# The last row of the last forgetting pair: squares moved by transfers between SBUF partitions instead of turns on TensorE

## The chip, the cores and the metric

The kernel runs on one core of a Trainium2 chip. A core has five engines with a queue of instructions each: TensorE (PE) for matrix products, VectorE (DVE), ScalarE (ACT), GpSimd (POOL) and SyncE (SP), which issues most transfers. Each engine takes its instructions in order and waits on semaphores for the others. Matrix products land in PSUM banks; everything else lies in SBUF, 128 partitions wide. The metric is the device time of one execution in microseconds.

## The reference

One layer of a streaming-encoder trunk on 512 tokens of 1024 channels in float32: four parallel token mixers, cross-attention into 256 memory tokens, and a gated MLP. The four mixers read one normalized input, their outputs are projected, gated and summed. The change touches mixer B, the forgetting attention with 8 heads of 64 channels:

```python
log_f = jax.nn.log_sigmoid(f_g + b_fgt)
c = jnp.cumsum(log_f, axis=1)
s = jnp.einsum('bqhd,bkhd->bhqk', q_blk, k) * scale
s = s + c_blk[..., None] - c_k[:, :, None, :]
p = jax.nn.softmax(jnp.where(mask, s, -jnp.inf), axis=-1)   # mask: key not later than query
o = jnp.einsum('bhqk,bkhd->bqhd', p, v)
```

The scores and the softmax have the queries on the partitions and the keys along the row. The product with the values sums over the keys, so TensorE needs the probabilities with the keys on the partitions. Turning them over, block by block, is what the change is about.

## The kernel before

Everything that stays exact to float32 is computed with split operands: a value is cut into a high half (a rounded copy, ScalarE) and a low half (the rest, VectorE), and a product is three matmuls, high by high, high by low and low by high (`mm3`). Weights go the same way: a raw tile `wr` (two buffers) is loaded by SyncE, split into `wh` and `wl` (four buffers each), lines 201 and 202, and used by one job. `run_blocks` goes through a list of jobs and emits the load and split of a job's weights three jobs ahead of its products.

The eight heads are done in four pairs. `f_task` of a pair is a generator with numbered steps. Steps 0 to 3 each do one row of 128 queries for both heads: scores on TensorE into two PSUM banks (`ps_sc`), the bias added on VectorE, the exponential on ScalarE, the scaling by the reciprocal sum (line 1141 on VectorE for one head, line 1143 on ScalarE for the other). Row r has (r + 1) times 128 keys. Tiles `e` with three buffers hold these rows and also their turned copies.

A row is turned in one of two ways:

- By way of DRAM. `turn_squares` transposes each 32 by 32 square in place of its block (VectorE, line 857), `put` writes the tile to DRAM (line 862), and `get` reads it back with block rows and partitions exchanged (line 869), which puts the keys on the partitions. The result lands in the low half's tile, and `split_in_place` (lines 875 and 876) cuts it into the tiles `pth` and `ptl`. All rows go this way but one.
- By the identity. `to_keys_major` turns each 128 by 128 block by a matrix product with the identity on TensorE (line 250, bank `ps_tr`), and `split` (lines 164 and 165) cuts the bank into the two tiles. Only row 3 of the last pair goes this way, in step 4.

`values` (in two halves, rows 0 and 1, then rows 2 and 3) multiplies the turned probabilities with the values into two banks `ps_av`; then lines 1155 and 1156 add the two parts and a split writes the pair's slice of the tile `y`, which the last branch reads. For rows 0 and 1 of the last pair the turned tiles are named `half`.

The order of the work: the list of jobs sets the order in which the program emits its main work. Background tasks such as `f_task` are advanced by a planner between blocks of matmuls: a step has a cost that is paid out of a credit, and a due time (its rest) before which the next step isn't taken. At the end of the mixer jobs `bg.drain("f")` takes all steps still left one after the other, whatever their rests. The pairs wait for each other: the last pair's step 4 waits until the pair before has done step 7. The compiler's scheduler then orders each engine's queue by its own timeline, so jobs that are emitted later can fill an engine while a step waits. After the drain come the jobs of the last branch: two gates (products of the normalized input with gate weights, tile names `hth` and `htl`), then a branch product with `y`, and so on in that rhythm. A PSUM bank for a job is taken in turn from a list of tags; `share_now("mm")` in step 4 of the last pair takes the bank `tr0` out of that list so that the turns can have it, and a later `share("mm", "av")` sets the list anew.

Of the kernel before, what the change touches and what calls it, by code (L numbers as in the profile page):

```python
# [17 lines left out]
F32 = mybir.dt.float32  # L18
# [68 lines left out]
def hybrid_layer(ctx: ExitStack, tc: tile.TileContext, a: dict, out: bass.AP):  # L87
    nc = tc.nc
    V, A, G, PE, SP = nc.vector, nc.scalar, nc.gpsimd, nc.tensor, nc.sync
# [10 lines left out]
    def bank(tag=None):  # L100
        if tag is None:
            turn_of.n += 1
            tag = turn_of.among[turn_of.n % len(turn_of.among)]
        elif tag == "tr":
            turn_of.tr = 1 if "tr0" in turn_of.among else 1 - turn_of.tr
            tag = f"tr{turn_of.tr}"
        return psum.tile([P, 512], F32, tag=tag, name=f"ps_{tag}", bufs=1 if tag[:2] == "tr" else 2)

    def share_now(*among):
        vars(turn_of).update(n=1, among=among)  # L110
# [29 lines left out]
    for i in range(8):  # L140
        n = ("wh", "wl")[i % 2]
# [3 lines left out]
        elif i < 6:  # L145
            n = ("fz_raw", "fz", "fe", "fu", "fd")[i - 1]
# [14 lines left out]
    def split(ps, hi, lo, scale=None):  # L161

        if scale is None:
            A.copy(hi, ps)  # L164
            V.tensor_tensor(lo, ps, hi.bitcast(F32), ALU.subtract)
        else:
            A.activation(hi, ps, AF.Copy if isinstance(scale, float) else AF.Identity, scale=scale)
            V.scalar_tensor_tensor(lo, ps, scale, hi.bitcast(F32), ALU.mult, ALU.subtract)
# [80 lines left out]
    def transpose(ps, x, n=P):  # L249
        turns.append(PE.transpose(ps, x, ident[:n, :n]).ins)  # L250
        bg.clock += 0.107
# [137 lines left out]
    for i, plan in enumerate(plans):  # L389
        r_t = m1p.tile([P, P], F32, tag="fbias" if i == 2 else "ck", name=f"rows{i}", bufs=2)  # L390
        n = 0
# [45 lines left out]
    turned = {}  # L437
# [401 lines left out]
    def to_keys_major(e, n, pt, local):  # L839

        ps = bank("tr")
        for kt in range(n):
            transpose(ps[:, kt * P:(kt + 1) * P], e[:, kt * P:(kt + 1) * P])
        split(ps[:, :n * P].rearrange("p (t a i) -> p a t i", t=n, a=4), *(x[:, local, :, :n] for x in pt))
# [14 lines left out]
    def put(e, w):  # L859
        d = dram.tile([2, P * S], F32, tag="turned", name="turned", bufs=6)[:e.shape[1], :P * w]  # L860
        d = d.rearrange("h (p x) -> p h x", p=P)
        SP.dma_start(d, e[:, :, :w])
        return d

    def part_of(pt, n, local):
        return pt[:, local, :, :n].rearrange("p a t i -> p a (t i)")

    def get(d, n, pt, local):
        SP.dma_start(part_of(pt[1], n, local).bitcast(F32), d.rearrange("(a j) (b x) -> (j b) a x", j=32, b=4))

    def split_in_place(n, pt, local):
        hi, lo = (part_of(x, n, local) for x in pt)
        raw = lo.bitcast(F32)
        with tc.issue_after(evacuations[0]):
            A.copy(hi, raw)  # L875
        V.tensor_tensor(lo, raw, hi.bitcast(F32), ALU.subtract)  # L876
# [24 lines left out]
    GETS, SPLITS = {3: (0, 1), 5: (2, 3)}, {4: (0, 1), 6: (2, 3)}  # L901
# [151 lines left out]
    def f_task(p, qk, v):  # L1053
        f_steps[p] = 0
        last = p == 3
        while f_steps[p - 1] < 4:
            yield 0.0, 0.5
        ck = []
        for j in range(2):
            t = m1p.tile([P, S], F32, tag="ck", name="ck", bufs=2)  # L1060
            G.dma_start(t, crows[2 * p + j:2 * p + j + 1, :].rearrange("a s -> (a s)").partition_broadcast(P))
            ck.append(t)
        yield 0.0, 2.0 if p else 5.0
        if "f" not in y:
            y["f"] = (y8(), y8())
        es, pts, av, ready = {}, {}, None, []
        gets, splits, rests, ends = ({4: (2,)}, {4: (0, 1), 5: (2,)}, {3: 2.0}, (5, 6)) if last else (GETS, SPLITS, {5: 6.5}, (5, 7))

        def fetch(qt):
            d = es.pop(qt)  # L1070
            for j in range(2):
                get(d[:, j], qt + 1, pts[qt // 2][j], qt % 2)

        def own_tiles():

            free = m1p.tile([P, 6, S], F32R, tag="qk", name="half", bufs=2)
            return [tuple(free[:, 2 * j + i].rearrange("p (l a t i) -> p l a t i", l=2, a=4, t=2) for i in range(2))
                    for j in range(2)]

        def turn_ready():  # L1080
            while ready:
                qt, e, w = ready.pop()
                turned = e4()
                for j in range(2):
                    turn_squares(turned[:, j, :w], e[:, j, :w])
                es[qt] = put(turned, w)
        for step in range(ends[1] + 1):
            if step in ends:
                if av is None:
                    av = [bank("av"), bank("av")]  # L1090
                with tc.issue_after(steps_of[0]):
                    for j in range(2):
                        hl = v[0][:, :, 2 * p + j]
                        half = ends.index(step)
                        values(av[j], lambda kt: ((hl[:, kt], 0), (hl[:, kt], 1)), pts[half][j], half)
            while step == (4 if last else 3) and f_steps[p - 1] < 8:
                yield 0.0, 0.5
            f_steps[p] = step + 1
            cost = 0.0
            if step == 4:  # L1100
                turn_ready()
            for qt in splits.get(step, ()):
                for j in range(2):
                    split_in_place(qt + 1, pts[qt // 2][j], qt % 2)
                cost += 0.1 + 0.3 * qt
            for qt in gets.get(step, ()):
                if qt % 2 == 0:
                    pts[qt // 2] = [pt_tiles() for _ in range(2)]
                fetch(qt)
            if step == 4 and last:  # L1110
                share_now("mm")
                e = es.pop(3)
                for j in range(2):
                    to_keys_major(e[:, j], 4, pts[1][j], 1)
                cost += 1.3
            if step < 4:
                qt, w = step, (step + 1) * P
                e = es[qt] = e4()
                st = m1p.tile([P, 8], F32, tag="st8", name="st8", bufs=4)
                for j in range(2):  # L1120
                    head = 2 * p + j
                    bias = m1p.tile([P, S], F32, tag="fbias", name="fbias", bufs=2)

                    G.tensor_scalar(bias[:, :w], ck[j][:, :w], -1.0, cq[:, qt, head:head + 1],
                                    ALU.mult, ALU.add)
                    G.affine_select(out=bias[:, w - P:w], in_=bias[:, w - P:w], pattern=[[-1, P]],
                                    compare_op=ALU.is_ge, fill=BIG, base=0, channel_multiplier=1)
                    ps = bank("sc")
                    scores(ps, qk, j, qt * P, w)
                    low = V.tensor_tensor_reduce(e[:, j, :w], ps[:, :w], bias[:, :w], scale=-HD ** -0.5,  # L1130
                                                 scalar=3.0e38, op0=ALU.add, op1=ALU.min,
                                                 accum_out=st[:, j:j + 1])
                with tc.issue_after(low.ins):
                    turn_ready()
                for j in range(2):
                    A.activation(e[:, j, :w], e[:, j, :w], AF.Exp, bias=st[:, j:j + 1],
                                 scale=-1.0, accum_out=st[:, 4 + j:5 + j])
                V.reciprocal(st[:, 6:8], st[:, 4:6])
                for j in range(2):
                    if j:  # L1140
                        V.tensor_scalar(e[:, j, :w], e[:, j, :w], st[:, 6 + j:7 + j], None, ALU.mult)
                    else:
                        A.activation(e[:, j, :w], e[:, j, :w], AF.Copy, scale=st[:, 6 + j:7 + j])
                cost += 0.6 + 0.0038 * w
                if not last or qt < 3:
                    ready.append((qt, e, w))
                    cost += 0.003 * w
                if last and qt == 2:
                    pts[0] = own_tiles()
                    fetch(0)  # L1150
                    fetch(1)
            yield cost, rests.get(step, 4.5)
        e = e4()
        for j in range(2):
            A.copy(e[0:HD, j], av[j][HD:P])
            V.tensor_tensor(e[j * HD:(j + 1) * HD, 0], av[j][0:HD], e[0:HD, j], ALU.add)
        split(e[:, 0], y["f"][0][:, p], y["f"][1][:, p])
        yield 1.8, 0.0
# [746 lines left out]
```

## Time and profile before

| | us |
|---|---|
| median of 3 runs (lowest, highest) | 1041.73 (1041.63, 1043.34) |
| the profiled execution | 1040.96 |
| its span, first to last instruction | 1039.2 |
| mean granted TensorE clock | 0.998 |

| engine | busy us | share of the span |
|---|---|---|
| TensorE, matmuls | 1029.6 | 99% |
| TensorE, weight loads | 876.3 | 84% |
| VectorE | 819.5 | 79% |
| ScalarE | 510.9 | 49% |
| GpSimd | 153.2 | 15% |

The shares are means over the whole run. TensorE's matmuls overlap each other in the array, so the time that one takes off the queue is read from the starts of neighbours rather than from its duration. A row of the timeline has the start in microseconds from the first instruction, the duration, the engine, the line, the operation with the tiles it writes and reads, its shape and how many like it were merged; in brackets stands how long the engine was idle before it and what ended that.

### The profile page before, as it was taken

The page shows a single profiled execution, that of the slowest core. Times are in us where ns is not written, and L with a number is a line of the kernel's source. Part 1 is how long each engine was busy: PE and PEld are TensorE (multiplying, and loading weights), DVE is VectorE, ACT ScalarE, POOL GpSimd, SP SyncE. Part 2 cuts the span into 40 slices and gives each one's busy share as a digit, 9 for nine tenths or more (in the row PEclk, how much of TensorE's full clock was granted, in tenths as well). Part 3 has the DMA queues.
Part 4 walks back from the last instruction along what each step waited for, and adds up shares of the span by engine and source line. Part 5 has one row for each costly group of instructions (what it writes and reads, how often), then busy time and mean ns, then how long its engine had stood idle before and what let it go on. Part 6 is the DMA issues. An engine that isn't in the chain of part 4 may idle for free.

```text
span 1039.2 us, 14390 instructions
## 1 busy us (share of the span) xinstructions
PE 1029.6 (99%) x5189; PEld 876.3 (84%) x5189; DVE 819.5 (79%) x1263; ACT 510.9 (49%) x838; POOL 153.2 (15%) x235
## 2 busy tenths in 40 slices
PE   9999999999999999999999999999999999999997
PEld 8888888888888988888888899898888888888886
DVE  7999999577788668878687898767777767667796
ACT  5322222376565465765634566645333433445672
POOL 4001000100020214342000021121112121111002
PEclk9999999999999999999999999999999999999999
DMA  8954333334534345766467744145677676625662
GB/s 272 320 155 97 102 102 102 83 100 114 150 99 131 88 131 167 203 172 168 143 199 251 239 137 123 46 138 166 199 239 235 211 236 207 213 82 191 216 212 82
DMA packets 194125, 169.36 MB, mean 163 GB/s; under 512 B 25295, under 2 KB 165692, under 8 KB 194053
## 3 DMA queue, kind: packets, MB, share of 16 engines
q1 hardware_dynamic: 185011, 136.69, 43.9%
q10 hardware_dynamic: 6482, 23.21, 6.1%
q0 software_dynamic: 2560, 8.54, 2.8%
q8 instruction: 41, 0.67, 0.3%
q14 instruction: 31, 0.25, 0.1%
HBM read 142.18 MB, written 26.23 MB: 162 GB/s over the span
## 4 chain that ended last, share of the span: by engine, by line
PE 96%; DMA 2%; DVE 1%; ACT 0%; issue 0%; SPq 0%; POOL 0%; POOLq 0%; DVEq 0%; ACTq 0%
PE ps_mm L244 46%; PE ps_av L244 30%; PE ps_tr L244 11%; PE ps_sc L244 7%; PE ps_tr L250 1%; DMA turned<-e 1%; DMA ptl<-turned 1%; PE ps_mm L462 1%; PE ps_av L462 1%; DMA xs<-in_x 0%; DVE e L857 0%; DVE e L939 0%; DVE e L930 0%; PE ps_tr L446 0%; DVE wl L202 0%
## 5 line engine op out<-in xcount | busy, mean ns | idle before, releaser
L201 ACT CAST wh<-wr 128x1024 fp32r<-128x1024 f32 (+1 forms) x140 | 146.3, 1047 | 235.3 <-PE ps_mm L244 119.3
L202 DVE TENSOR_TENSOR wl<-wr,wh 128x1024 fp32r<-128x1024 f32 (+1 forms) x140 | 175.1, 1251 | 83.1 <-ACT wh L201 81.2
L244 PE MATMUL ps_mm<-hth,wh 128*128 128x512 f32 (+1 forms) x536 | 198.3, 377 | 0.0
L244 PE MATMUL ps_mm<-htl,wh 128*128 128x512 f32 (+1 forms) x536 | 198.3, 377 | 0.0
L244 PE MATMUL ps_mm<-hth,wl 128*128 128x512 f32 (+1 forms) x536 | 198.1, 377 | 0.0
L244 PE MATMUL ps_av<-htl,wh 128*128 128x512 f32 (+1 forms) x328 | 122.5, 373 | 0.0
L244 PE MATMUL ps_av<-hth,wh 128*128 128x512 f32 (+1 forms) x328 | 122.4, 373 | 0.0
L244 PE MATMUL ps_av<-hth,wl 128*128 128x512 f32 (+1 forms) x328 | 122.3, 373 | 0.0
L244 PEld LDWEIGHTS ps_mm<-hth,wh 128*128 128x128 f32 x536 | 99.1, 188 | 18.3 <-ACT hth L164 0.3
L244 PEld LDWEIGHTS ps_mm<-hth,wl 128*128 128x128 f32 x536 | 98.9, 188 | 18.2
L244 PEld LDWEIGHTS ps_mm<-htl,wh 128*128 128x128 f32 x536 | 99.0, 188 | 18.0
L697 DVE SCALAR_TENSOR_TENSOR y<-y,par,y 128x508 f32<-128x508 f32 (+29 forms) x120 | 82.8, 731 | 0.1
L244 PEld LDWEIGHTS ps_av<-hth,wl 128*128 128x128 f32 x328 | 61.7, 188 | 11.0
L244 PEld LDWEIGHTS ps_av<-htl,wh 128*128 128x128 f32 x328 | 61.5, 188 | 10.9
L244 PEld LDWEIGHTS ps_av<-hth,wh 128*128 128x128 f32 x328 | 61.6, 188 | 10.8
L1696 DVE TENSOR_TENSOR wl<-dw,wh 128x1024 fp32r<-128x1024 f32 x32 | 40.2, 1261 | 16.8 <-ACT wh L1695 16.6
L1695 ACT CAST wh<-dw 128x1024 fp32r<-128x1024 f32 x32 | 33.5, 1052 | 24.5 <-PE ps_tr L244 10.1
L1643 ACT ACTIVATE th<-c 128x512 f32<-128x512 f32 x22 | 13.9, 632 | 48.6 <-DVE c L624 48.6
L624 DVE SCALAR_TENSOR_TENSOR c<-ps_mm,par,c 128x510 f32<-128x510 f32 (+1 forms) x44 | 32.7, 744 | 0.7
L857 DVE STREAM_TRANSPOSE e<-e 128x128 f32<-128x128 f32 (+3 forms) x46 | 32.5, 729 | 0.2
L876 DVE TENSOR_TENSOR ptl<-ptl,pth 128x384 fp32r<-128x384 f32 (+3 forms) x42 | 20.7, 511 | 14.9 <-ACT pth L875 14.8
L244 PE MATMUL ps_tr<-htl,wh 128*128 128x512 f32 x80 | 31.7, 396 | 0.0
(518 smaller groups left out, 2238.5 us busy)
## 6 DMA issues: line engine op xcount, KB each, us to landing
wr<-in_w_up SPq DMA_DIRECT2D x44, 512.0 KB
wr<-in_w_in SPq DMA_DIRECT2D x38, 512.0 KB
wr<-in_w_gate SPq DMA_DIRECT2D x32, 512.0 KB
wp<-in_w_down ACTq DMA_DIRECT2D x22, 512.0 KB
sums<-wp ACTq DMA_DIRECT2D x22, 512.0 KB
dw<-sums SPq DMA_DIRECT2D x44, 256.0 KB
wr<-in_w_branch SPq DMA_DIRECT2D x16, 512.0 KB
wide<-in_w_out SPq DMA_DIRECT2D x12, 512.0 KB
```

The costliest lines, as they stand in the source:

```text
L201: last_weights[:] = [order(A.copy(hi, raw[:, :n])).ins, low.tensor_tensor(lo, raw[:, :n], hi.bitcast(F32), ALU.subtract).ins]
L202: low.tensor_tensor(lo, raw[:, :n], hi.bitcast(F32), ALU.subtract).ins]
L244: steps_of[:] = [PE.matmul(ps, lhs, rhs, start=start, stop=stop).ins]
L250: turns.append(PE.transpose(ps, x, ident[:n, :n]).ins)
L462: keep(PE.matmul(banks[c][:, :S // 2], w[p == 1][:, k, c * P:(c + 1) * P], ht[p == 2][:, i * 4 + k, :S // 2], start=(i, p, k) == (0, 0, 0) ...
L624: ins = V.scalar_tensor_tensor(dst[:, s:], src[:, :S - s], w(k), dst[:, s:], ALU.mult, ALU.add)
L697: ins = V.scalar_tensor_tensor(dst[:, s:], src[:, :S - s], pc("conv_dw", k * 4 + j), dst[:, s:], ALU.mult, ALU.add)
L857: V.transpose(dst, src.rearrange("p (t j b) -> p b t j", b=4, j=32))
L876: V.tensor_tensor(lo, raw, hi.bitcast(F32), ALU.subtract)
L1643: A.activation(th, c[:, 0], AF.Silu)
L1695: A.copy(hi, x)
L1696: V.tensor_tensor(lo, x, hi.bitcast(F32), ALU.subtract)
```

## The change

Row 3 of the last pair no longer goes to TensorE. Its squares are transposed on VectorE like those of the other rows, and a new function `move` then exchanges block rows and partitions by transfers straight from one SBUF tile to another, four for each head, one for each block row of 32 partitions, each of 64 KB. There is no trip through DRAM for this row. The two splits of row 3 become splits in place. They stand in step 6 with those of row 2, the second half of the values moves from step 6 to step 7, and step 5 gets a rest of its own. In step 4, the turning comes after the splits of rows 0 and 1 and the gets of row 2. The call that takes `tr0` out of the list of banks is gone.

```diff
+    def move(e, n, pt, local):
+
+        dst = part_of(pt[1], n, local).bitcast(F32)
+        for a in range(4):
+            SP.dma_start(dst[:, a], e[a * 32:(a + 1) * 32].rearrange("j (b x) -> j b x", b=4))
...
-        gets, splits, rests, ends = ({4: (2,)}, {4: (0, 1), 5: (2,)}, {3: 2.0}, (5, 6)) if last else (GETS, SPLITS, {5: 6.5}, (5, 7))
+        gets, splits, rests, ends = ({4: (2,)}, {4: (0, 1), 6: (2, 3)}, {3: 2.0, 5: 6.0}, (5, 7)) if last else (GETS, SPLITS, {5: 6.5}, (5, 7))
...
                 for j in range(2):
                     turn_squares(turned[:, j, :w], e[:, j, :w])
-                es[qt] = put(turned, w)
+                if last and qt == 3:
+                    for j in range(2):
+                        move(turned[:, j], 4, pts[1][j], 1)
+                else:
+                    es[qt] = put(turned, w)
...
-            if step == 4:
+            if step == 4 and not last:
                 turn_ready()
...
             if step == 4 and last:
-                share_now("mm")
-                e = es.pop(3)
-                for j in range(2):
-                    to_keys_major(e[:, j], 4, pts[1][j], 1)
-                cost += 1.3
+                turn_ready()
...
-                if not last or qt < 3:
-                    ready.append((qt, e, w))
-                    cost += 0.003 * w
+                ready.append((qt, e, w))
+                cost += 0.003 * w
```

## The prediction

> **What bounds the kernel now.** I read the page first: the busy times, then the chain that ended last.
>
> ```profile
> span 1039.2 us, 14390 instructions
> PE 1029.6 (99%) x5189; PEld 876.3 (84%) x5189; DVE 819.5 (79%) x1263; ACT 510.9 (49%) x838; POOL 153.2 (15%) x235
> PE 96%; DMA 2%; DVE 1%; ACT 0%; issue 0%; SPq 0%; POOL 0%; POOLq 0%; DVEq 0%; ACTq 0%
> ```
>
> TensorE is the bound nearly everywhere: 1029.6 of 1039.2 us busy, 96% of the chain. So a change pays what it takes off TensorE's list and costs each hole it makes in it. The stretches of time around the tail of the last forgetting pair (columns: stretch, its length, then PE, PEld, DVE, ACT, POOL busy with counts, granted clock, DMA share, GB/s) show no hole there today, at the full clock:
>
> ```profile
> 488.00:500.49 12.49, 12.49 (x64) 10.54 (x63) 11.72 (x28) 8.35 (x19) 2.86 (x4) 1.00 0.47 134
> 500.49:512.45 11.96, 11.96 (x69) 10.45 (x68) 7.09 (x10) 7.22 (x13) 1.31 (x3) 1.00 0.73 209
> ```
>
> Next TensorE's instructions in order of time (start, duration, operation):
>
> ```profile
> 474.56 0.28 PE L244 MATMUL ps_av<-pth,v 128*128 128x256 f32 x1
> ...
> 475.43 0.61 PE L244 MATMUL ps_sc<-qk 128*128 128x128 f32 x4
> ...
> 487.13 0.40 PE L244 MATMUL ps_mm<-y8b,wl 128*128 128x512 f32 x1
> 487.37 0.87 PE L244 MATMUL ps_sc<-qk 128*128 128x384 f32 x4
> ...
> 500.49 0.60 PE L250 MATMUL ps_tr<-ident,e 128*128 128x128 f32 x4
> 500.85 0.49 PE L244 MATMUL ps_av<-half,v 128*128 128x256 f32 x2
> 501.18 0.60 PE L250 MATMUL ps_tr<-ident,e 128*128 128x128 f32 x4
> 501.53 0.88 PE L244 MATMUL ps_av<-half,v 128*128 128x128 f32 x6
> 502.25 0.44 PE L244 MATMUL ps_mm<-hth,wh 128*128 128x512 f32 x1
> ...
> 503.69 0.62 PE L244 MATMUL ps_mm<-y,wh 128*128 128x512 f32 x2
> ...
> 505.76 0.28 PE L244 MATMUL ps_av<-pth,v 128*128 128x256 f32 x1
> ...
> 507.59 0.46 PE L244 MATMUL ps_mm<-hth,wh 128*128 128x512 f32 x1
> ...
> 512.45 0.62 PE L244 MATMUL ps_av<-y,wh 128*128 128x512 f32 x2
> ```
>
> The last product of the first branch (from tile y8b) ends at 487.37, and the third score row of the last pair (384 keys) stands right behind it. No first-branch block is left, so everything the pair does from its step 3 on is emitted by the drain, one step after the other. The new rests and due times (5: 6.0, one step more) therefore move nothing: nobody waits for them. What fills TensorE beside the drain is the last branch: its gates 0 and 1 up to 503.69, then the first block's products with the three ready slices of y (nine matmuls up to 505.76), the second half of the values up to 507.59, and from there gate 2.
>
> **Part 1, off TensorE.** The eight turns lie in two groups of four, 0.36 and 0.35 us from start to next start. The whole piece 500.49 to 502.25 is 1.76 us; the same eight value products of the pair before, alone, took 474.56 to 475.43, 0.87. So the eight turns cost 0.71 to 0.89 us; I take 0.89, which includes the switching between them. With it gone the nine products end at 505.76 - 0.89 = 504.87.
>
> A turn's own duration is another number:
>
> ```profile
> L250 PE MATMUL ps_tr<-ident,e x8: 270/272/273, 500.5 to 501.5; 128*128 128x128 f32 x8
> ```
>
> They overlap, since four fit into 0.36 us. The Trainium skill, page "TensorE: Matmul & The Clock Gate", section "Part 4: PE-mode transpose", gives about 275 ns for a transpose in a kernel; the duration agrees, and eight times it would be an estimate of 2.2 us saved, where the starts give 0.89.
>
> **Part 2, onto VectorE.** Two stream transposes of 128x512, priced by the only group that holds this shape alone (duration in ns, least, median, most):
>
> ```profile
> L857 DVE STREAM_TRANSPOSE m_t<-mn x4: 1036/1062/1087, 522.1 to 541.3; 128x512 f32<-128x512 f32 x4
> ```
>
> VectorE's present work at this place:
>
> ```profile
> 486.38 0.68 DVE L876 TENSOR_TENSOR ptl<-ptl,pth 128x512 fp32r<-128x512 f32 x1
> ...
> 499.21 0.42 DVE L876 TENSOR_TENSOR half<-half 128x256 fp32r<-128x256 f32 x1
> 500.14 1.23 DVE L202 TENSOR_TENSOR wl<-wr,wh 128x1024 fp32r<-128x1024 f32 x1 [0.51 <-ACT wh L201]
> 501.36 0.69 DVE L165 TENSOR_TENSOR y<-e,y 128x512 fp32r<-128x512 f32 x1
> ...
> 504.38 1.29 DVE L165 TENSOR_TENSOR ptl<-ps_tr,pth 128x512 fp32r<-128x512 f32 x2
> ...
> 506.23 1.23 DVE L202 TENSOR_TENSOR wl<-wr,wh 128x1024 fp32r<-128x1024 f32 x1
> ...
> 509.78 0.69 DVE L165 TENSOR_TENSOR y<-e,y 128x512 fp32r<-128x512 f32 x1 [0.69 <-ACT y L164]
> ```
>
> and ScalarE's (the second row is the scaling of row 3, head 0):
>
> ```profile
> 484.89 0.62 ACT L875 CAST pth<-ptl 128x512 fp32r<-128x512 f32 x1 [0.54 <-DMA ptl<-turned]
> ...
> 498.13 0.73 ACT L1143 ACTIVATE e<-e,st 128x512 f32<-128x512 f32 x1
> ...
> 503.35 0.51 ACT L875 CAST pth<-ptl 128x384 fp32r<-128x384 f32 x1 [2.03 <-DMA ptl<-turned]
> 503.77 1.07 ACT L164 CAST pth<-ps_tr 128x512 fp32r<-128x512 f32 x2
> ...
> 505.14 1.06 ACT L201 CAST wh<-wr 128x1024 fp32r<-128x1024 f32 x1
> ```
>
> Row 3 is scaled at 498.86, VectorE is free at 499.63, before the low half of the next weights can start (500.14). So I take the transposes first: 2 x 1.06, 499.63 to 501.75. Behind them stands the low half wl, 501.75 to 502.98 instead of 500.14 to 501.37, then the pair before's y. The block that reads this wl begins at 503.69 - 0.89 = 502.80, so about 0.2 us shows; it vanishes in the wait of part 5.
>
> **Part 3, the evacuation.** Two copies out of PSUM on ScalarE (1.07 for both) and two subtractions on VectorE (1.29 for both) become two splits in place, 0.62 and 0.68 each: 0.2 us more work on two engines that idle here (ScalarE 2.03 ahead of 503.35), so nothing on the path beyond what part 6 counts.
>
> **Part 4, SyncE's queue.** It issues in order. Today:
>
> ```profile
> 496.73 0.36 SPq L862 DMA_DIRECT2D turned<-e  x1
> 499.24 0.91 SPq L869 DMA_DIRECT2D ptl<-turned  x2
> 501.39 0.37 SPq L185 DMA_DIRECT2D wr<-in_w_gate  x1
> ...
> L869 SPq DMA_DIRECT2D ptl<-turned x2: 360/403/446, 499.2 to 499.7; - x2
> ```
>
> The load of gate 2's weights leaves at 501.39, right when wl (end 501.37) has freed its buffer. After the change eight moves come ahead of it in program order, 0.40 us each by the gets' mean: the first four from 500.69, when head 0 is transposed, to 502.29, the others to 503.89. The load can leave at 503.89 instead of 501.39: 2.50 later.
>
> **Part 5, what waits for that.** Today from the load's issue to the end of gate 2's low half (506.23 + 1.23) are 6.07 us, and gate 2 starts 0.13 later, at 507.59: just in time, hidden behind the nine products and the values. After: 503.89 + 6.07 + 0.13 = 510.09. The bound from below: the put of row 2 had landed 2.51 us after its issue (496.73 to 499.24), so with 2.5 for landing, 1.06 and 1.23 for the two halves, 508.7, that is 1.1 late. I take 2.5, since the DMA engines are 0.73 busy there and 512 KB of moves go ahead of the load.
>
> **Part 6, do the values come before that?** The nearest landing times:
>
> ```profile
> crows<-e POOLq DMA_DIRECT2D x1, 16.0 KB, 1.9
> ```
>
> 1.9 us for 16 KB, and 4.1 for row 2's gets (issue 499.24, first use 503.35). Head 0's last move starts at 501.89, head 1's at 503.49; landed 503.8 to 506.0 and 505.4 to 507.6; with 0.62 + 0.68 for the split, ready 505.1 to 507.3 and 506.7 to 508.9. The values take 1.83 (505.76 to 507.59), half per head, so they end by 509.8 at the latest, ahead of gate 2. The Trainium skill, page "DMA: Bandwidth & Descriptors", section "Anatomy of one DMA — SWDGE (gpsimd) path", puts a transfer at 2.0 us fixed plus bytes by 436 GB/s: an estimate of 2.15 us for 64 KB; that lies within the two rows and leaves the sum as it is.
>
> So TensorE's nine products end at 504.87, it does 1.83 us of values somewhere in the wait, and goes on with gate 2 at 510.09 instead of 507.59: the 0.89 us is swallowed by the wait. Other work for the hole would be the block's second product, whose bank is freed by the pair's last evacuation; today that product stands behind all of gate 2, at 512.45, so I count no cover. The pair's y is ready 2.88 us after the values (507.59 to 510.47), so 512.7 at the latest, and today it is read after 512.45: that moves by 2.5 too. Without the claim of PSUM bank sharing gate 0 may take another bank; TensorE does not wait there (first stretch above): nothing.
>
> Sum: +2.5 us. The profiled execution is 1040.96 us, 0.77 below the median 1041.73; so 1043.5 by it, 1044.2 at the median. Its own range is +1.9 to +4, 1043.6 to 1045.7. 0.2%, about what a measurement of this kernel can tell from no change, is 2.08 us.
>
> **Rivals.**
>
> Rival 1, hidden or nearly (chance 0.32). wl keeps its place at 500.14 and the load its place at 501.39, the transposes come behind them, 501.37 to 503.49. Gate 2 starts on time at 507.59; the values come later and leave a hole 504.87 to 507.46 for the nine products' successor, less the first head's 0.9 us if it is ready by then: +0.9 to +1.8, or with every wait covered -0.89. Time 1040.8 to 1043.6, middle 1042.6. For it: wl is emitted earlier than the row's transposes. Against: it is ready 0.5 us later.
>
> Rival 2, faster (0.08). The place is the piece from 500.49: the turns are worth their full duration, 8 x 0.272 = 2.18 us, and what follows moves up by that: 1039.5. It decides from 0.26 us per turn on, where eight are worth 2.08. For it: the duration in the row. Against: four starts within 0.36 us, which is 0.09 each. The skill's 275 ns says the same as the duration.
>
> Rival 3, much slower (0.14). The order on TensorE puts the values ahead of gate 2 and the moves land at twice the slower row, 8.2 us, on busy DMA engines behind the second rather than the first transpose: 503.49 + 8.2 + 1.3 = 513.0, values to 513.9, gate 2 there instead of at 507.59: +6.3, 1048.
>
> **How the numbers follow.** Forecast 0.46, rival 1 0.32, rival 2 0.08, rival 3 0.14. Slower by over 0.2%: forecast and rival 3 less the edge of the forecast, 0.58; within: rival 1 and that edge, 0.34; faster 0.08. The range 1041.0 to 1047.5 leaves out rival 2, a few hundredths of rival 1's lower end and part of rival 3.
>
> **What would show it.** TensorE has an idle stretch between 504 and 510, released by gate 2's wl or by the splits; the gate load on SyncE's queue leaves 2 to 3 us later, behind eight moves of about 0.4 us; two transposes of about 1.06 stand ahead of wl. Wrong would be: no idle on TensorE there (rival 1 or 2), a load at its old place, or order shifts far from this place.

## The result and the profile after

The changed kernel takes 1049.74 us (median of 4 runs, 1048.73 to 1050.44) against 1041.68 us of the kernel before in the same measurement: ratio 1.0073, 95% interval 1.0056 to 1.0091, 8.06 us slower. The profiled execution of the changed kernel is 1050.01 us.

The page after; the third line is the share of each engine in the chain that ended last:

```profile
span 1048.2 us, 14393 instructions
...
PE 1033.1 (99%) x5181; PEld 877.2 (84%) x5181; DVE 821.1 (78%) x1265; ACT 511.1 (49%) x838; POOL 154.9 (15%) x235
...
PE 95%; DMA 2%; DVE 1%; ACT 0%; issue 0%; SPq 0%; POOL 0%; POOLq 0%; DVEq 0%; ACTq 0%
```

The span grew by 9.0 us, TensorE's busy time by 3.5, though it has eight turns less to do. So there is idle time, and part of the rest runs slower. The place is found by two marks that both kernels have: the third score row of the last pair (384 keys), and the first product of the joined mixers (`ps_sc<-wh,mix`). Between them lies all that the change touches. The columns are those of the prediction's stretches; first before, then after, the whole and three pieces of it:

```profile
487.37:560.05 72.68, 72.68 (x345) 61.04 (x344) 52.96 (x82) 34.59 (x54) 7.23 (x13) 1.00 0.57 176
```

```profile
488.42:568.96 80.54, 74.64 (x337) 61.67 (x336) 56.45 (x86) 35.15 (x54) 7.93 (x13) 0.96 0.55 164
...
505.00:508.35 3.35, 1.09 (x5) 0.56 (x3) 1.12 (x2) 1.02 (x2) 0.00 (x0) 1.00 0.96 250
508.35:511.50 3.15, 0.00 (x0) 0.00 (x0) 0.01 (x1) 0.66 (x2) 0.00 (x0) 0.64 0.98 306
511.50:516.28 4.78, 4.62 (x14) 3.80 (x15) 3.19 (x4) 2.58 (x4) 0.00 (x0) 0.52 0.41 116
```

The stretch is 7.86 us longer, close to the measured loss of 8.06. Another 1.05 us of the profiled span lie ahead of the first mark (488.42 against 487.37) and are not the change's: in the profiled executions of the experiments that mark lies anywhere from 487.22 to 489.31. In the stretch TensorE was never idle before; now it is idle for 80.54 - 74.64 = 5.90 us. Behind the idle time the granted clock is 0.52: 4.62 us of matmuls at that rate are 4.62 x 0.48 = 2.2 us longer than at the full one (an estimate, and an upper one, since the first of them ended in a short wait anyway). With the 0.86 us of the turns off (shown below) that makes 5.90 + 2.2 - 0.86 = 7.3; 0.6 us stay unassigned. In the text below "the stretch" is the time between these two marks.

TensorE around the hole, in order of time, and ScalarE at its end:

```profile
505.70 0.39 PE L244 MATMUL ps_mm<-y,wl 128*128 128x512 f32 x1
511.51 0.58 PE L244 MATMUL ps_av<-pth,v 128*128 128x256 f32 x1 [5.42 <-ACT pth L881]
...
513.79 0.73 PE L244 MATMUL ps_mm<-hth,wh 128*128 128x512 f32 x1
...
530.74 0.73 PE L244 MATMUL ps_mm<-y,wh 128*128 128x512 f32 x2 [0.33 <-DVE ge L1190]
```

```profile
510.84 0.62 ACT L881 CAST pth<-ptl 128x512 fp32r<-128x512 f32 x1 [4.60 <-DMA ptl<-e]
511.37 1.04 ACT L201 CAST wh<-wr 128x1024 fp32r<-128x1024 f32 x1
```

The nine products end at 506.09, and then TensorE waits 5.42 us, not for weights, but for the split of row 3, head 0. ScalarE itself had waited 4.60 us for the moves. On TensorE the values stand ahead of gate 2. On ScalarE this split stands ahead of the high half of a later block's weights (511.37) and of the activation of gate 1 at 512.31, which reads a bank `ps_mm`; two experiments below show gate 2 waiting for that activation. So a late split holds up both.

The chain of waits in this place (start, duration, what) and SyncE's queue, then the group of the eight moves (duration in ns, least, median, most):

```profile
502.63 1.70 SPq L875
...
504.37 0.60 SPq L875
...
505.02 5.72 DMA ptl<-e
```

```profile
501.92 6.33 SPq L875 DMA_DIRECT2D ptl<-e  x8
508.35 5.72 SPq L185 DMA_DIRECT2D wr<-in_w_gate  x2
```

```profile
L875 SPq DMA_DIRECT2D ptl<-e x8: 544/617/1695, 501.9 to 507.6; - x8
```

The eight moves hold SyncE for 6.33 us, one of them for 1.70, and from the last move of head 0 (505.02) to its landing are 5.72 us. The DMA engines are 0.96 to 0.98 busy meanwhile, with 250 to 306 GB/s (the two pieces from 505.00 to 511.50 above). What else they carry, beside the weights that SyncE loads from 508.35 on, is on GpSimd's queue: the loads of the norm's gain and the first memory tokens, 512 KB each:

```profile
503.80 0.57 POOL L1273 DMA_DIRECT2D g_mem<-in_norm_mem  x1 [10.12 <-PE ps_mm L244]
504.37 0.54 POOL L1307 DMA_DIRECT2D m_t<-in_mem  x1
```

VectorE did what was expected: two transposes, and the low half of a later job's weights right behind them:

```profile
500.81 2.07 DVE L857 STREAM_TRANSPOSE e<-e 128x512 f32<-128x512 f32 x2
502.81 1.17 DVE L202 TENSOR_TENSOR wl<-wr,wh 128x1024 fp32r<-128x1024 f32 x1
```

### The profile page after: what moved, and what is told of

Its sections match the earlier page's. It is cut to its first block, busy times and chain, and to the rows that moved or that the text cites. A ratio compares the mean times of both kernels' runs of the same rounds, so it can differ in the third digit from the quotient of the medians.

```text
span 1048.2 us, 14393 instructions
## 1 busy us (share of the span) xinstructions
PE 1033.1 (99%) x5181; PEld 877.2 (84%) x5181; DVE 821.1 (78%) x1265; ACT 511.1 (49%) x838; POOL 154.9 (15%) x235
## 4 chain that ended last, share of the span: by engine, by line
PE 95%; DMA 2%; DVE 1%; ACT 0%; issue 0%; SPq 0%; POOL 0%; POOLq 0%; DVEq 0%; ACTq 0%
PE ps_mm L244 44%; PE ps_av L244 29%; PE ps_tr L244 11%; PE ps_sc L244 7%; PE ps_tr L250 1%; DMA ptl<-turned 1%; DMA turned<-e 1%; PE ps_mm L462 1%; DMA ptl<-e 1%; PE ps_av L462 1%; DVE e L857 0%; DMA half<-turned 0%; PE ps_sc L408 0%; PE ps_mm L403 0%; SPq L875 0%
## 5 line engine op out<-in xcount | busy, mean ns | idle before, releaser
L244 PE MATMUL ps_mm<-htl,wh 128*128 128x512 f32 (+1 forms) x528 | 195.8, 378 | 0.0
L244 PE MATMUL ps_mm<-hth,wh 128*128 128x512 f32 (+1 forms) x528 | 195.6, 378 | 0.0
L244 PE MATMUL ps_mm<-hth,wl 128*128 128x512 f32 (+1 forms) x528 | 195.2, 377 | 0.0
L881 ACT CAST pth<-ptl 128x384 fp32r<-128x384 f32 (+3 forms) x44 | 19.5, 466 | 31.6 <-DMA ptl<-turned 25.6
L244 PE MATMUL ps_tr<-htl,wh 128*128 128x512 f32 x88 | 34.8, 395 | 0.0
L244 PE MATMUL ps_tr<-hth,wh 128*128 128x512 f32 x88 | 34.8, 395 | 0.0
```

Of the source, the lines that this page charges most:

```text
L244: steps_of[:] = [PE.matmul(ps, lhs, rhs, start=start, stop=stop).ins]
```

## The experiments

Three theories were on the table. **Q** is the prediction's own: gate 2's weight load, queued behind the moves on SyncE, sets the end. **L**: the landing of row 3's moves sets it, since the values stand ahead of gate 2. **C**: a part of the loss is the lower clock that follows the hole. A diff is against the changed kernel where nothing else is said.

### Row 3 by way of DRAM, no moves

```diff
-                if last and qt == 3:
-                    for j in range(2):
-                        move(turned[:, j], 4, pts[1][j], 1)
-                else:
-                    es[qt] = put(turned, w)
+                es[qt] = put(turned, w)
```

with the gets of row 3 in step 5 (a line that is left out here).

> Edit: the changed kernel, but row 3 goes by DRAM like all other rows (one put, two gets in step 5) instead of by eight moves; here the gate load stands ahead of the two gets on SyncE's queue. Theory Q (the prediction's: gate 2's weights, queued behind the eight moves, set when TensorE goes on): the load leaves at once, gate 2's weights are there by about 508, so about 1045. Theory L (the row itself lands late, and the product with the values, which stands ahead of gate 2 in TensorE's order, holds everything): put 2.5 us plus gets 4.1 us after the transposes' end at 502.9 gives values at about 511, as after the change: 1048 to 1051.

1048.09 us (1046.69 to 1048.98), ratio 1.0062 [1.0049, 1.0075]. SyncE, ScalarE and TensorE:

```profile
503.40 0.57 SPq L185 DMA_DIRECT2D wr<-in_w_gate  x1
506.48 0.99 SPq L869 DMA_DIRECT2D ptl<-turned  x2
```

```profile
513.33 0.62 ACT L881 CAST pth<-ptl 128x512 fp32r<-128x512 f32 x1 [6.07 <-DMA ptl<-turned]
```

```profile
507.31 0.50 PE L244 MATMUL ps_mm<-hth,wh 128*128 128x512 f32 x1 [1.81 <-ACT ge L1174]
...
518.86 1.05 PE L244 MATMUL ps_av<-y,wh 128*128 128x512 f32 x2 [1.99 <-DVE e L1157]
```

The gate load that stood behind the moves leaves at 503.40, five microseconds earlier, and in the order that the compiler chose here gate 2 goes ahead of the values. 6.45 of the 8.06 us are still lost: the row is split at 513.33 only, and TensorE waits at two other places, 1.81 us for the activation of gate 1 and 1.99 us for the sum behind the values (line 1157). A row that is late in another way costs nearly the same, so the moves themselves are not special.

### Gate 2's load on ScalarE's queue

```diff
-        order(SP.dma_start(t.rearrange("p (k c) -> p k c", k=shape[1]) if len(shape) == 3 else t, src))
+        order((queue or SP).dma_start(t.rearrange("p (k c) -> p k c", k=shape[1]) if len(shape) == 3 else t, src))
...
+                if (n, m0 + i) == (1, 2):
+                    yield lambda c=c: split_weights(*load_raw(*c, queue=A)), None, f
```

> Edit: the changed kernel, with the one load of gate 2's weights issued by ScalarE instead of SyncE, so that it no longer queues behind the eight moves. Theory Q (the load's place in the queue sets the end): it leaves at about 504 instead of 508, gate 2 can start 4 us earlier, 1045 to 1046. Theory L (row 3's landing sets the end): the hole still ends on the row's split; the load now shares the DMA engines with the moves from their start, so the split comes no earlier: 1049 to 1051.

1049.06 us (1047.14 to 1050.95), ratio 1.0068 [1.0054, 1.0082]: no different from the changed kernel. The profiled execution is the fastest of the four, 1047.14. First the loads on ScalarE's and on SyncE's queue, then the chain, and TensorE:

```profile
478.14 0.42 ACTq L185 DMA_DIRECT2D wr<-in_w_gate  x1
```

```profile
506.46 5.04 SPq L185 DMA_DIRECT2D wr<-in_w_gate  x2
```

```profile
503.11 5.06 DMA ptl<-e
```

```profile
508.94 0.39 PE L244 MATMUL ps_av<-pth,v 128*128 128x256 f32 x1 [3.76 <-ACT pth L881]
```

The edit marks gate 2's load by its queue, and so shows where it really is: it leaves at 478.14, some 22 us ahead of the moves, and SyncE still issues a gate load right behind them, at 506.46. That second load belongs to a later gate. So the run does not take a load out from behind the moves; it shows that gate 2's load never stood there. In the kernel before, SyncE's load in the same place of its order is this one:

```profile
477.92 0.79 SPq L185 DMA_DIRECT2D wr<-in_w_gate  x1
```

Counting on from it (gate 2, gate 3, a branch block, gate 4), the load that leaves at 501.39 there, and at 508.35 after the change, is gate 4's. The splits say the same. Each load has one split, in the same order, and the two loads from 501.39 on are split only here, since the split after these two, at 524.10, waits for the branch load of 520.78:

```profile
515.82 2.00 ACT L201 CAST wh<-wr 128x1024 fp32r<-128x1024 f32 x2 [3.68 <-PE ps_av L244]
```

Theory Q falls with this, not by the time of the run: in the stretch of the changed kernel TensorE waits for no weights (5.42 us for the row's split, 0.33 for VectorE at 530.74), so the delay of gate 4's load costs nothing there.

### The memory tokens' loads after the moves

```diff
+                    if last and (qt, j) == (3, 1):
+                        mark = m1p.tile([P, 8], F32, tag="st8", name="mark", bufs=4)
+                        ns.landed = G.tensor_copy(mark[:, :1], pts[1][1][0][:, 1, 0, 0, :1].bitcast(F32)).ins
...
+            with tc.issue_after(ns.landed):
+                G.dma_start(m_t, mem_d[t * P:(t + 1) * P, :])
```

and the same for the load of the gain.

> Edit: the changed kernel, but the two 512 KB loads of the memory tokens' gain and first rows, issued by GpSimd, wait until row 3 of the second head has landed (a one-element copy on GpSimd reads it first). Theory L with contention: the moves share the 16 DMA engines with these loads and the gate load (share 0.96 to 0.98 in that stretch); without 1 MB of it they land 2 us or more earlier, the hole on TensorE falls from 5.4 to about 3 us and the clock stays up: 1045 to 1047. Theory L without contention (a move lands late by itself): as after the change, 1049 to 1050. Theory Q: the gate load still leaves behind the moves, no more than 1 us better.

1044.64 us (1043.12 to 1045.64), ratio 1.0026 [1.0015, 1.0037]: 5 of the 8 us are gone. The chain, then TensorE:

```profile
503.53 2.14 DMA ptl<-e
```

```profile
506.44 0.39 PE L244 MATMUL ps_av<-pth,v 128*128 128x256 f32 x1 [1.56 <-ACT pth L881]
```

With the two 512 KB loads out of the way the last move of head 0 lands in 2.14 us instead of 5.72, and the hole shrinks from 5.42 to 1.56 us. The moves were the same, on the same queue (5.79 us for the eight). With the loads in place it is 5.06 to 6.41 us in the four profiled executions with all eight moves on SyncE whose chain shows it. So the landing was long because moves and loads shared the DMA engines. The Trainium skill, page "DMA: Bandwidth & Descriptors", section "Issuing engines are not separate DMA queues", says that transfers of any issuing engine run on the same 16 engines and interleave; 5.72 against 2.14 us agrees, as it was GpSimd's loads that slowed SyncE's moves.

### The moves on GpSimd's queue

```diff
-            SP.dma_start(dst[:, a], e[a * 32:(a + 1) * 32].rearrange("j (b x) -> j b x", b=4))
+            G.dma_start(dst[:, a], e[a * 32:(a + 1) * 32].rearrange("j (b x) -> j b x", b=4))
```

> Edit: the changed kernel, but the eight moves are issued by GpSimd; SyncE's queue is then free for the gate load, and the token loads stand behind the moves on GpSimd's queue. Theory Q: the gate load leaves at about 504, gate 2's weights are ready by 508 to 509, 1044 to 1046. Theory L: the hole on TensorE still ends on the first head's split, shorter only by what the moves land earlier (issue 0.55 each instead of 0.62 to 1.7, and no token loads beside them): 1046 to 1048, and the releaser of the hole stays the row's split.

1043.89 us (1043.20 to 1045.06), ratio 1.0022 [1.0013, 1.0031]. GpSimd's queue, the chain and TensorE:

```profile
501.41 4.38 POOL L875 DMA_DIRECT2D ptl<-e  x8 [8.66 <-DVE e L857]
505.68 0.65 POOL L1273 DMA_DIRECT2D g_mem<-in_norm_mem  x1
```

```profile
503.05 3.08 DMA ptl<-e
```

```profile
506.75 0.50 PE L244 MATMUL ps_mm<-hth,wh 128*128 128x512 f32 x1 [1.58 <-ACT ge L1178]
```

One edit does several things: the moves leave GpSimd ahead of the tokens' loads (which wait behind them until 505.68), SyncE's queue is free, and the compiler puts gate 2 ahead of the values, as by way of DRAM. The landing is 3.08 us. How much is due to which was not tried apart. The hole that is left, 1.58 us, is ended by ScalarE's activation of gate 1 (506.02 to 506.70), and no longer by the row. In the kernel before that activation ended at 506.79, and nobody saw it, because TensorE had the turns and the values to do until 507.59.

### One head moved, the other turned on TensorE

Head 1 goes by the moves, head 0 by the four turns as before the change (its split and the call for the bank, left out here, are as before too).

```diff
-                    for j in range(2):
-                        move(turned[:, j], 4, pts[1][j], 1)
+                    move(turned[:, 1], 4, pts[1][1], 1)
...
+                to_keys_major(es.pop(3)[:, 0], 4, pts[1][0], 1)
```

> Edit: only the second head of row 3 goes by moves (four of them), the first is turned on TensorE by the identity as before. Theory L with contention: four moves leave within about 3 us, the gate load follows 3 us earlier than in the changed kernel, 256 KB less are in the way; the first head's values fill 0.9 us of the hole. About half of the loss: 1044 to 1046. If the loss came from the planner's edits or the freed bank rather than from the moves, it would stay at 1048 to 1050.

1046.35 us (1041.67 to 1049.27 in ten runs), ratio 1.0040 [1.0023, 1.0057]. SyncE:

```profile
500.84 2.94 SPq L875 DMA_DIRECT2D ptl<-e  x4
```

Half the moves, a good half of the loss by the median (4.66 us), but the runs differ by 7.6 us: three, with a mean granted clock of 0.998 over the run, take 1041.67 to 1042.98, the others, at 0.995 to 0.997, take 1046.17 to 1049.27. In the profiled one (1046.18) the hole is 2.81 us and the landing of the last move 5.38. It looks as if the row lands in time in some executions and not in others, and the clock follows; only one of them has a trace, so this is not shown.

### Useless matmuls in the hole

First twelve matmuls behind the nine products, that is between the third and the fourth slice of the first block:

```diff
...
+                            if k == 2:
+                                for _ in range(12):
+                                    with tc.issue_after(steps_of[0]):
+                                        matmul(spare, hl[0][:, 2], y[key][1][:, 2], True, True)
...
```

> Edit: the changed kernel, with 12 matmuls of no use (2.7 us, into a spare bank) in the hole on TensorE, behind the third slice of y and ahead of the values. They shorten the idle time from 5.4 to about 2.7 us and delay nothing. Theory C (part of the loss is the clock, which is granted at 0.5 from 509.2 to 516 after 3.3 us of idleness): the clock stays at 1.0, the matmuls behind the hole take 0.23 instead of 0.43 us, about 2 us faster than the changed kernel, 1047.5 to 1048. Rival: the clock drop costs nothing, since something else (weights, evacuation) sets the pace there: no change, 1049.7.

1048.69 us (1045.64 to 1050.23), ratio 1.0067 [1.0054, 1.0079]. A hole of 2.99 us is left behind them, and the clock falls from 513.0 to 516.5. That is inconclusive, since TensorE still idles. So a second version, with 27 matmuls in that place:

```diff
+                    if last and (qt, j) == (2, 1):
+                        spare = bank("tr")
+                        for _ in range(27):
+                            matmul(spare[:, :384].rearrange("p (a x) -> p a x", a=4), v[0][:, 0, 2 * p], part_of(pts[1][1][1], 3, 0), True, True)
```

> The changed kernel with 27 useless matmuls of 384 columns in TensorE's order between the first block's nine products and the values of the last pair; they read row 2's squares, split at 506.85 in the changed kernel's trace, and so run from about 506.9 to about 511.6, the time at which the values can start there. The result does not depend on them. Theory C (about 2.2 us of the loss are matmuls at half the granted clock, and the clock falls because TensorE idled for more than 5 us): the hole shrinks to about 1 us, the granted clock stays at 1.00 through 509 to 517, the values start at 511.5 as before, and the kernel is 2.2 us faster than the changed one, 1047.5. If the clock falls for another reason (the transfers, or any hole of a microsecond): it stays at 0.5 for 3.4 to 7 us, and the time at 1049.7 or a little above.

1048.04 us (1047.76 to 1049.11), ratio 1.0064 [1.0051, 1.0078]. TensorE, and two pieces of time:

```profile
505.29 5.03 PE L244 MATMUL ps_tr<-ptl,v 128*128 128x384 f32 x27
510.61 0.38 PE L244 MATMUL ps_av<-pth,v 128*128 128x256 f32 x1 [0.28 <-ACT pth L881]
```

```profile
510.32:513.00 2.68, 1.78 (x10) 1.27 (x9) 2.16 (x3) 2.66 (x5) 0.00 (x0) 1.00 0.30 78
513.00:516.60 3.60, 3.22 (x12) 2.89 (x12) 1.64 (x3) 0.84 (x3) 0.00 (x0) 0.53 0.52 146
```

The hole is filled. Four of the five runs have a mean clock of 0.998, like the kernel before, and take 1047.76 to 1048.14; the fifth, which is the profiled one, has 0.996 and takes 1049.11. All four runs of the changed kernel lie at 0.994 to 0.997. The loss is 6.5 us here (1048.04 against 1041.56) and 8.06 in the changed kernel: the difference of 1.6 us has about the size that theory C gives, 2.2 at most by the sum above. It is not proved by this. The intervals of the two ratios overlap, the compiled order differs in one more place (the second head's values stand ahead of gate 2 here), and the four runs at 0.998 left no trace, so their clock is known by its mean only. In the profiled one the clock falls at 513.2 all the same, though TensorE lacks only 0.90 us of the 2.68 up to 513.0, in short waits for the splits of the two heads, and its stretch is as long as in the changed kernel (80.65 us against 80.54). So a hole of five microseconds, as theory C had it, isn't needed for the drop. The other 6.5 us would then be the wait for the row, here spent on useless work.

### Work to cover the hole

The second block of the last branch gets a free bank, so that its nine ready products (2.0 us) stand ahead of the values:

```diff
-                    ps = bank()
+                    ps = bank("tr" if (n, m) == (1, 1) else None)
```

> Edit: the changed kernel (moves on SyncE) with only that second edit, 2.0 us of cover on TensorE. Theory L: the hole shrinks from 5.4 to about 3.4 us, still long enough for the clock to drop: 1047 to 1048. If something other than lack of work holds TensorE, no change: 1049.7.

1046.24 us (1044.51 to 1047.91), ratio 1.0046 [1.0031, 1.0062]. The hole is 1.62 us, where 3.4 were expected, still ended by the row's split, behind a landing of 5.27 us. 2.0 us of cover gained 3.5 by the medians. In the profiled execution, the fastest of the four, the clock is low for 3.4 us instead of 6.9, and SyncE is done with the moves in 5.18 us instead of 6.33; so the cover may not be the only reason. Together with the moves on GpSimd's queue:

> Edit: the moves are issued by GpSimd (as in the run before with that edit, 1043.9), and the first last-branch block's second product takes its bank from the turns' banks, which are free now, instead of waiting for the pair's own bank: 2.0 us more work that TensorE can do while the row is on its way. Theory: what is left of the loss there is the 1.6 us hole; with 2.0 us of cover it closes, and 0.89 us of turns is saved: 1041 to 1042, no slower than before the change. Rival: the hole is only moved behind the cover, since gate 2's weights or its bank end it: 1043.5 to 1044.

1041.80 us (1040.50 to 1045.00), ratio 1.0003 [0.9994, 1.0012]. The stretch, and TensorE later:

```profile
487.96:559.78 71.82, 71.82 (x337) 60.22 (x336) 53.40 (x82) 32.66 (x51) 11.55 (x21) 1.00 0.57 170
```

```profile
563.07 0.50 PE L244 MATMUL ps_mm<-wh,mix 128*128 128x512 f32 x1 [0.40 <-ACT ge L1178]
...
566.31 0.50 PE L244 MATMUL ps_mm<-wh,mix 128*128 128x512 f32 x1 [0.36 <-DVE ge L1190]
```

No hole and no drop of the clock are left in the profiled execution, and by the median the whole loss is gone; two of the eleven runs, with a mean clock of 0.997, still take 1044.67 and 1045.00. Here too gate 2 goes ahead of the values. The stretch is 0.86 us shorter than before: that is what the turns were worth. It isn't seen in the time; in the profiled execution two small holes come behind the stretch, 0.76 us together. Why was not tried. The cover alone, put into the kernel before:

> The kernel before with one edit only: the last branch's second block goes to the free bank, so that its ready products come earlier in TensorE's order. It tells what of the version with the moves by GpSimd and this cover (stretch from the third score row to the last branch's first mix product 71.82 us, against 72.68 before) comes from the missing turns and what from the cover. If the cover alone gains nothing, since TensorE has no hole there before the change: 1041.6, ratio 1.000, stretch 72.7, and the 0.86 us are the turns. If the cover itself gains: stretch 71.8 to 72.3, and the turns were worth less than 0.86.

1040.85 us (1040.34 to 1041.59) against 1042.38 of the kernel before in that measurement, ratio 0.9987 [0.9978, 0.9996]: 0.4 to 2.3 us less, about the 0.2% that a measurement of this kernel can tell. Nothing of it is in the stretch, which is unchanged (72.69 against 72.68), so the 0.86 us there are the turns and not the cover:

```profile
488.38:561.07 72.69, 72.69 (x346) 61.06 (x344) 54.43 (x84) 34.88 (x54) 7.20 (x13) 1.00 0.58 173
```

An attempt to keep the 0.86, with head 0's moves on GpSimd's queue, head 1's on ScalarE's, and the cover:

```diff
-                        move(turned[:, j], 4, pts[1][j], 1)
+                        move(turned[:, j], 4, pts[1][j], 1, (G, A)[j])
```

> Moves by GpSimd for head 0 and by ScalarE for head 1, and the last branch's second block taken to a free bank so that its nine ready products (2.0 us) stand ahead of the values. With the moves by GpSimd alone and this cover there was no hole and the stretch around the change was 0.86 us shorter than before, but the token loads on GpSimd's queue left later and about 1 us was lost after 560. Here four moves leave GpSimd's queue, so the token loads leave about 2 us earlier. If those late loads were the cost: 1040.8, 0.9 us below before, ratio 0.9992. If ScalarE's own queue is held up by its four moves (0.6 us each, 2.4 us, ahead of the next weights' split): a hole of up to 2.4 us returns and the time is 1042 to 1044.

1043.54 us (1042.51 to 1044.54), ratio 1.0021 [1.0012, 1.0030]. The chain, then TensorE:

```profile
504.15 6.77 DMA ptl<-e
```

```profile
511.69 0.38 PE L244 MATMUL ps_av<-pth,v 128*128 128x256 f32 x1 [0.89 <-ACT pth L881]
```

The tokens' loads do leave earlier, at 503.92, and the landing, now of head 1's last move on ScalarE's queue, is back at 6.77 us. The time is that of the second expectation, but not for its reason: ScalarE sat idle for 3.75 us ahead of the row's split, waiting for the landing. No version of the change is faster than the kernel before.

### The turns twice

The kernel before with eight more turns, into a bank that nobody reads:

```diff
+                    turn_only(e[:, j], 4)
                     to_keys_major(e[:, j], 4, pts[1][j], 1)
```

> The kernel before with the eight turns of the row emitted twice: the second set goes into a PSUM bank that nobody reads, so nothing of the result depends on it. It prices the turns alone. If eight turns cost 0.71 to 0.89 us on TensorE (their starts), the time is 0.7 to 0.9 us above before, ratio about 1.0008. If they cost their full durations, 8 x 0.272, it is 2.2 us above, ratio 1.0021; then the change should have saved 2.2 us where it is made, and the loss to explain is 10.2 us and not 8.9.

1043.04 us (1042.09 to 1044.21), ratio 1.0015 [1.0006, 1.0023], that is 0.6 to 2.4 us, which by itself doesn't decide. The eight that stand together, and the stretch:

```profile
503.59 1.03 PE L250 MATMUL ps_tr<-ident,e 128*128 128x128 f32 x8
504.38 0.88 PE L244 MATMUL ps_av<-half,v 128*128 128x128 f32 x6
```

```profile
489.31:562.89 73.58, 73.58 (x353) 61.94 (x352) 53.78 (x82) 34.99 (x54) 7.22 (x13) 1.00 0.54 165
```

Eight turns take 0.79 us from start to next start, and the stretch is 0.90 us longer than before. By the stretch, the full durations (2.2 us) are out.

## Why the prediction was wrong

The direction was right and the size wrong: +8.06 us where the sum had +2.5, outside the range. The wait that the 2.5 stood for does not exist, so that the direction came out is in part luck. Parts 5 and 6 are the steps that failed.

**Part 1** (0.71 to 0.89 us off TensorE) was right: 0.86 in the stretch where nothing else waits, 0.90 when doubled. The Trainium skill's about 275 ns for a transpose ("TensorE: Matmul & The Clock Gate", "Part 4: PE-mode transpose") match the duration here, 0.272 us; the starts show 0.10 us for each turn on the queue, and they decided rightly.

**Part 2** was right about VectorE: two transposes, 2.07 us, ahead of wl. **Part 3** named the cost of the splits rightly as work, but not their place. ScalarE takes its queue in order, and the split of the late row stands ahead of the activation that gate 2 needs.

**Part 4** had the order right and the size wrong: the moves took SyncE 6.33 us and not 3.2, 0.62 by the median and one 1.70, where the gets' 0.40 had been carried over. The load behind them left at 508.35, 5.9 us later than before when the 1.05 us ahead of the stretch are taken off, instead of 2.5.

**Part 5 is the first step that failed: it had the wrong wait.** The load at 501.39 was read as gate 2's, and the split that ends at 507.46 (506.23 + 1.23) as the split of that load. They do not belong together. Gate 2's load leaves at 477.92; the load at 501.39 is gate 4's and is split at 515.82; the split at 505.14 is that of the branch block's load at 492.50. That gate 2 starts 0.13 us behind the end of that split is a coincidence: TensorE had no gap there, the values ended then. The lead of three jobs, by which loads go ahead of their products, speaks against the reading. The 0.2 us of part 2 rest on the same pairing.

**Part 6 is the second: it had the landing too short.** It took 1.9 to 4.1 us from issue to landing, from a 16 KB transfer and from row 2's gets, and concluded that the values come in time. Measured were 5.72 us. Head 0's row was split at 512.18, or 511.13 less the 1.05 ahead of the stretch, against 507.3 at the latest: 2.1 us of the difference come from the issues (part 4), 1.6 from the landing. The prediction never listed what else would be on the DMA engines at that time, the two 512 KB loads on GpSimd's queue; without them the same moves land in 2.14 us. The kernel before shows these loads, in the list of its issues from 498 to 512 (KB each, median us to landing):

```profile
g_mem<-in_norm_mem POOLq DMA_DIRECT2D x1, 512.0 KB, 6.9
m_t<-in_mem POOLq DMA_DIRECT2D x1, 512.0 KB, 7.6
```

**The term that was missing** is the clock: about 2 us of matmuls at half rate behind the hole, an estimate that the runs support and do not prove.

**No cover** was counted, and none was there. Gate 2 could not have filled the hole from its start either: the activation of gate 1, which it waits for in two of the experiments, ended at 506.79 before the change. The planner's new rests were counted at nothing, and no run tries them alone; with the moves on GpSimd's queue and the cover they are still in, and the loss is gone. Gate 0 took another bank, as the prediction allowed, and TensorE did not wait there.

**Rivals.** Rival 3 (much slower, 0.14) had the mechanism: values ahead of gate 2 in TensorE's order, and a long landing on busy DMA engines. Its landing of 8.2 us was too long, so gate 2 came 5.15 us late (513.79 against 507.59, less the 1.05 ahead of the stretch) and not 6.3. Most of the other 2.7 us of the stretch come behind that: the second head's values, which now stand behind gate 2 (0.9), the clock, which no rival had (some 1.2 from there on), and the 0.33 us at 530.74. Rival 1 (hidden) and rival 2 (turns at full duration) fell, the first by the hole, the second by the turns' starts.

## What to carry to other kernels

Before a late load is priced, count loads, splits and products to see which product it feeds; two rows that end close together need not belong together. Before a transfer is priced, list what every other queue will have in flight in the same microseconds, and take the landing from a row under that load. Then look at the in-order queues of the engines that consume it, since what stands behind the consumer waits too. A product of less than a microsecond is no good trade for a transfer that TensorE's next instruction waits for, unless there is ready work to put ahead of it.

## What was not expected of the hardware

**The clock.** In the profiled executions each drop of the granted clock is to 0.5 for 3.4 us (in the changed kernel twice that, 509.2 to 516.1), and it begins up to 2.2 us after a hole has ended (with the cover alone: 509.29, then 511.5), or while TensorE still idles. With row 3 by way of DRAM, a hole of 1.81 us that ended at 507.31 is followed by this piece:

```profile
508.85:512.30 3.45, 3.45 (x10) 2.69 (x9) 0.00 (x0) 0.00 (x0) 0.00 (x0) 0.51 1.13 331
```

The moves on GpSimd's queue leave a hole of nearly the same length, 1.58 us, with no drop in the profiled execution. The Trainium skill, page "TensorE: Matmul & The Clock Gate", section "Part 1: The HAM clock gate (the "warmup" mystery)", describes a free-running window of 3413 ns, half the clock after at least one idle window and the full clock after a busy one. The length of the drops and their start at no fixed distance from the hole agree. That a whole idle window is needed doesn't: in the 3.4 us ahead of the drop TensorE idled for 1.81 us here, and with the 27 matmuls for about 1 us in pieces. How much idle time in a window brings the drop wasn't settled.

**The cost of issuing.** A 64 KB move between SBUF partitions held SyncE for 0.54 to 0.68 us; in five of the seven profiled executions with moves on SyncE the second one took 0.93 to 1.70, and in a sixth the first one 1.27, while row 2's gets of 192 KB took 0.36 to 0.45. Fewer bytes were not cheaper to issue. Why one move was slower wasn't tried.

**The scatter.** Kernels whose TensorE waits for a landing spread over up to 7.6 us between executions (one head moved), the kernel before over 1.6 to 2.6 in each measurement. What makes a landing come in time in one execution and not in the next stays open.
